# A decoder layer on one core: new byte offsets for six weight buffers in SBUF, and one buffer shared by two small tables

## The chip, the cores and the metric

The kernel runs on 1 NeuronCore of one Trainium2 chip. The metric is the device time of one execution in microseconds (us). The median of three runs of the kernel before is 2798.57 us (2797.53 to 2799.73).

## What is computed

One layer of a hybrid decoder on 512 tokens of width 2048, all in float32. Cut to what matters:

```python
mod = silu(c) @ w_ada + b_ada                      # six adaLN vectors of 2048
h = rmsnorm(x, g_mix) * (1 + sc1) + sh1
proj = h @ w_in                                    # 2048 x 11344
y_a = stick_breaking_attention(8 heads) @ w_a
y_b = dsa_attention(8 heads, top 128 keys by an indexer) @ w_b
x = x + (1 + gt1) * ((sigmoid(g_a) * y_a + sigmoid(g_b) * y_b) @ w_o)
h = rmsnorm(x, g_ffn) * (1 + sc2) + sh2
u = conv_b + causal depthwise conv of width 3 of (h @ w_up)     # 2048 x 11264
a, b = split(u)
x = x + (1 + gt2) * ((silu(a) * b) @ w_down)       # 5632 x 2048
out = rmsnorm(x, g_final)
```

## The kernel before

**Three matmuls for one product.** A float32 operand is split into a high part (rounded to the type `float32r` by a copy on ScalarE) and a low part (what is left, by a subtraction on VectorE). `mm3` (lines 164 to 168) then makes a product of two operands with three matmuls into the same PSUM tile: high by high (L166), high by low (L167), low by high (L168). Each matmul on TensorE (PE) has its own load of a stationary operand (LDWEIGHTS, the engine PEld in the profile) and streams a moving operand.

**The weights.** `load` (L143) brings 128 x 1024 elements of a weight matrix from HBM into one of eight `raw` buffers. `parts` (lines 152 to 159) splits it: L156 writes `wh`, L158 writes `wl`. There are three pairs of buffers, `wh0`/`wl0`, `wh1`/`wl1`, `wh2`/`wl2`; `turns` counts the calls of `parts` from 0, and call n uses pair n mod 3. A call's buffers are read by all matmuls of that block: 8 column groups of 128 for a block of 1024.

**The other operand.** Activations and what is formed of them lie in 62 slots named `F` of 512 elements (2048 bytes of each partition), split into high and low in the same way (L185, L187).

**Where the time is spent.** Most of the large matrix products run in `unit` (L230) with Strassen's scheme: two column blocks of 128 at a time, seven products in place of eight. One product is 8 blocks x 3 matmuls = 24 matmuls of 256 moving columns, `F` moving and a weight block of 128 x 128 stationary, and takes one call of `parts`. 31 units do most of the input projection, 8 the output projection `w_o`, 41 the up-projection `w_up`; the first part of the up-projection (`plain`, L1126) has the same matmuls at its own lines 1132 to 1134. Other products stream 512 columns: `proj` and the indexer's queries with the weights stationary, the values (L467 and `values`, L687) and the down-projection (`plain_down`, `strassen_down`) with the weights moving.

**Order.** Each engine runs its instructions in program order. ScalarE makes the high parts, the evacuations of PSUM and activation functions; VectorE makes the low parts, Strassen's sums and the adaLN products; SyncE issues the weight loads; GpSimd issues the saves and fetches of intermediate tiles.

**The layout in SBUF.** Tiles of the pool `sb` get their places in the order in which their tags are first seen, and each tile's room is a multiple of 32 bytes. The tables, the `F` slots and the `raw` buffers have sizes that are multiples of 128 bytes and all start at 0 modulo 128. Lines 127 to 140 ask for small tiles and weight buffers in turn, and so place the latter:

```python
eps = sb.tile([P, 1], F32, tag="eps", name="eps")       # 32 bytes of room
t2k("wh0", 1, F32R, 1024)                                # 32 modulo 128
inv = sb.tile([64, 1], F32, tag="inv", name="inv")      # 32 bytes
t2k("wh1", 1, F32R, 1024)                                # 64
sb.tile([P, NQB], F32, tag="r0", name=nm("r"))          # 32 bytes
t2k("wh2", 1, F32R, 1024)                                # 96
c_col = sb.tile([P, KT], F32, tag="c_col", name="c_col")  # 64 bytes
t2k("wl0", 1, F32R, 1024)                                # 32
...
```

and so on: `wl1` lies at 64 and `wl2` at 0. Modulo 128 bytes, and taken from the `F` slots, pair 0 lies at 32 (high) and 32 (low), pair 1 at 64 and 64, pair 2 at 96 and 0. A column group of 128 elements is 512 bytes and half an `F` slot is 1024 bytes, so every stationary block and every moving block starts at its buffer's offset modulo 128.

**The two small tables.** `macc` (L124) collects the adaLN sums, written by `ada_half` (L307) and read last by `ada_end` (L320) near the end of the output projection. `cw` (L123) holds the convolution's weights; its one DMA is issued from ScalarE's queue (L1105), and `conv` (L1108) reads it in the up-projection.

Of the kernel before, what the change touches and what calls it, by code (L numbers as in the profile page):

```python
# [10 lines left out]
F32 = mybir.dt.float32  # L11
F32R = mybir.dt.float32r
# [6 lines left out]
P = 128  # L19
# [57 lines left out]
def block_kernel(ctx: ExitStack, tc: tile.TileContext, A: dict, out: bass.AP):  # L77
    nc = tc.nc
    sb = ctx.enter_context(tc.tile_pool(name="sb", bufs=1))
    pp = ctx.enter_context(tc.tile_pool(name="pp", bufs=1, space=PSUM))  # L80
    dr = ctx.enter_context(tc.tile_pool(name="dr", bufs=1, space=bass.MemoryType.DRAM))

# [2 lines left out]
    def nm(s):  # L85
        counter[0] += 1
        return f"{s}_{counter[0]}"
# [4 lines left out]
    def slot(dt=F32):  # L92

        return t2k("F", SLOTS, dt)
# [14 lines left out]
    stt = nc.vector.scalar_tensor_tensor  # L109


    def small_r():
        counter[0] += 1
        return sb.tile([P, NQB], F32, tag=f"r{counter[0] % 2}", name=nm("r"))

    const = sb.tile([P, 5, P], F32, tag="const", name="const")
    ident, ones, negones, negtri, causal = (const[:, i, :] for i in range(5))
    vec = sb.tile([P, 96 + 2 * KT], F32, tag="vec", name="vec")
# [1 line left out]
    b_ada = vec[:, :96]  # L120
    g_mix, g_ffn = (vec[:, 96 + i * KT : 96 + (i + 1) * KT] for i in range(2))
    mask = sb.tile([P, 2, P], BF16, tag="mask", name="mask")
    cw = sb.tile([P, 2 * NJ, 4], F32, tag="cw", name="cw")  # L123
    macc = sb.tile([P, 96, 2], F32, tag="macc", name="macc")  # L124
    mod = sb.tile([P, 96], F32, tag="mod", name="mod")
    amp = sb.tile([P, 2, KT], F32, tag="amp", name="amp")
    slot()
    eps = sb.tile([P, 1], F32, tag="eps", name="eps")
    nc.vector.memset(eps, EPS)
    t2k("wh0", 1, F32R, 1024)  # L130
    inv = sb.tile([64, 1], F32, tag="inv", name="inv")
    t2k("wh1", 1, F32R, 1024)
    sb.tile([P, NQB], F32, tag="r0", name=nm("r"))
    t2k("wh2", 1, F32R, 1024)
    c_col = sb.tile([P, KT], F32, tag="c_col", name="c_col")
    t2k("wl0", 1, F32R, 1024)
    sb.tile([P, NQB], F32, tag="r1", name=nm("r"))
    t2k("wl1", 1, F32R, 1024)
    sb.tile([P, NQB], F32, tag="m", bufs=2, name=nm("m"))
    t2k("wl2", 1, F32R, 1024)  # L140


    def load(src, w=1024):  # L143
# [4 lines left out]
    pins = {}  # L148

    turns = [0]  # L150

    def parts(raw, w=1024):
        i = turns[0] % 3
        turns[0] += 1
        wh = t2k(f"wh{i}", 1, F32R, w)
        pins["wh"] = act(wh, raw, AF.Copy)  # L156
        wl = t2k(f"wl{i}", 1, F32R, w)
        pins["wl"] = tt(wl, raw, wh.bitcast(F32), ALU.subtract)  # L158
        return wh, wl

# [142 lines left out]
        return c1, c2  # L303

    def ada_half(cb, t, half, tag=("raw", 8)):  # L307
        raw = t2k(*tag, w=1024)
# [35 lines left out]
        return cb  # L344

    cb = c_spread()
    nc.scalar.dma_start(c_col, A["c_col"])
    act(c_col, c_col, AF.Silu)


    def rms(squares, blocks=range(NQB), bank=outs):

        total = bank()
        at = slice(blocks[0] * P, (blocks[-1] + 1) * P)
        for b in blocks:
            for i, t in enumerate(squares):
                mm(total[:, b : b + 1], t[:, b * P : (b + 1) * P], ones[:, :1], start=b == blocks[0] and i == 0,
                   stop=i == len(squares) - 1, skip_group_check=True)
        r = small_r()
        rb = r[:, blocks[0] : blocks[-1] + 1]  # L360
        act(rb, total[:, blocks[0] : blocks[-1] + 1], AF.Sqrt, scale=1.0 / D, bias=eps)
        nc.vector.reciprocal(rb, rb)
        wide = t2k("T", 2)
        for b in blocks:
            ts(wide[:, b * P : (b + 1) * P], ident, r[:, b : b + 1], None, ALU.mult)
        yield
        out = bank()
        mm(out[:, at], ones, wide[:, at], start=True, stop=True)
        yield out
# [138 lines left out]

    def rope_tables():
        f0, f1, f2, f3, f123, f23, fr = _turn_parts()  # L510
        nc.scalar.dma_start(inv, A["inv_freq"])
        pos = t2k("T", 2, I32)[:64]
        nc.scalar.dma_start(pos, A["positions"].to_broadcast([64, S]))
        turn = [t2k("w", 2)[:64] for _ in range(2)]

        def nearest(o, i, step):
            m = 1.5 * 2.0**23 * step
            ts(o, i, m, m, ALU.add, ALU.subtract)

        for half in range(2):  # L520
            at = slice(half * HALF, (half + 1) * HALF)
            q1, q2 = (t[:, at] for t in turn)
            tmp = sb.tile([P, 5 * HALF], F32, tag="soft", name=nm("soft"))[:64]
            ang, a2, a1, a0, rn = (tmp[:, i * HALF : (i + 1) * HALF] for i in range(5))
            nc.vector.tensor_copy(ang, pos[:, at])
            ts(ang, ang, inv, None, ALU.mult)
            nearest(a2, ang, 2.0**20)
            tt(ang, ang, a2, ALU.subtract)
            yield
            nearest(a1, ang, 2.0**8)  # L530
            tt(ang, ang, a1, ALU.subtract)
            nearest(a0, ang, 2.0**-4)
            tt(ang, ang, a0, ALU.subtract)
            small = ang
            ts(small, ang, fr, None, ALU.mult)
            yield
            stt(small, a0, f123, small, ALU.mult, ALU.add)
            stt(small, a1, f23, small, ALU.mult, ALU.add)
            stt(small, a2, f3, small, ALU.mult, ALU.add)
            ts(q1, a1, f0, None, ALU.mult)  # L540
            stt(q1, a2, f1, q1, ALU.mult, ALU.add)
            yield
            nearest(rn, q1, 1.0)
            tt(q1, q1, rn, ALU.subtract)
            ts(q2, a1, f1, None, ALU.mult)
            stt(q2, a2, f2, q2, ALU.mult, ALU.add)
            nearest(rn, q2, 1.0)
            tt(q2, q2, rn, ALU.subtract)
            yield
            stt(q1, a0, f0, q1, ALU.mult, ALU.add)  # L550
            tt(q1, q1, q2, ALU.add)
            nearest(rn, q1, 1.0)
            tt(q1, q1, rn, ALU.subtract)
            tt(q1, q1, small, ALU.add)
            yield
            nearest(rn, q1, 1.0)
            tt(q2, q1, rn, ALU.subtract)
            ts(q1, q2, 0.25, None, ALU.add)
            nearest(rn, q1, 1.0)
            tt(q1, q1, rn, ALU.subtract)  # L560
            yield
        TWO_PI = float(np.nextafter(np.float32(2 * np.pi), np.float32(0)))
        q1, q2 = turn
        for n, step in enumerate((64, 32)):
            o = t2k("raw", 8, w=1024)
            for i in range(P // step):
                at = slice(step * i, step * i + step)
                act(o[at, :S], q1[:step], AF.Sin, scale=TWO_PI)
                act(o[at, S:], q2[:step], AF.Sin, scale=TWO_PI if i % 2 else -TWO_PI)
                if i % 2:  # L570
                    yield
            save(rope_d[n], o)
# [140 lines left out]
    def indexer():  # L713
# [6 lines left out]
        for b in range(NQB):  # L720
            nc.tensor.transpose(wps[:, b * IDXH : (b + 1) * IDXH], tail[IDXD:TN, b * P : (b + 1) * P],
                                ident[IDXD:TN, IDXD:TN])
        wi = sb.tile([P, NQB, IDXH], F32, tag="wi", name="wi")
        nc.vector.tensor_copy(wi.rearrange("p b h -> p (b h)"), wps[:, : NQB * IDXH])
        bias.extend(slot()[:, : (b + 1) * P] for b in range(1, NQB))
        yield
# [36 lines left out]
        for b in range(1, NQB):  # L763
            sc = bias[b]
            for i in range(TOPK // 8):
                m8 = sb.tile([P, 8], F32, tag="m8", bufs=2, name=nm("m8"))
                nc.vector.max(out=m8, in_=sc)
                nc.vector.match_replace(out=sc, in_to_replace=m8, in_values=sc, imm_value=TAKEN)
                if i % 2:
                    yield  # L770
            ts(sc, sc, TAKEN, NEG, ALU.not_equal, ALU.mult)
# [127 lines left out]
    ya = [split(o) for o in ya]  # L899

    def sparse_1(q, k):
        m = sb.tile([P, NQB], F32, tag="m", bufs=2, name=nm("m"))
        s = sb.tile([P, NQB], F32, tag="s", bufs=2, name=nm("s"))
        soft = sb.tile([P, 10 * P], F32, tag="soft", name=nm("soft"))
        lg = strips(*(acc() for _ in range(3)))
        p = strips(*of_soft(soft))
# [125 lines left out]
    def norm_late(c1, c2):  # L1032
# [1 line left out]
        c, sq = (c1, c2), (t2k("ta", 2), t2k("sp", 2))  # L1034
        total, rstd = att(), outs()
        wide = t2k("T", 2)
        r = small_r()

        def add_up(t, blocks, first=False):
            for b in blocks:  # L1040
# [60 lines left out]
    rstd, finish_left, *left_norm = norm2  # L1101


    with behind(sig):
        nc.scalar.dma_start(cw, A["conv"])  # L1105
    yd = [dr.tile([P, 2 * S], F32, tag=f"yd{j}", name=f"yd{j}") for j in range(NJ // 2)]
# [349 lines left out]
        return [fetch(x1t[:, t, b * S : (b + 1) * S]) for b in range(2, 4)]  # L1456

    def finish_tokens(t, xs, s):
        r = small_r()
        tt(r[:, :2], s[:, :2], s[:, 2:], ALU.add)  # L1460
        tt(r[:, 2:3], r[:, :1], r[:, 1:2], ALU.add)
        act(r[:, 3:], r[:, 2:3], AF.Sqrt, scale=1.0 / D, bias=eps)  # L1462
        nc.vector.reciprocal(r[:, 3:], r[:, 3:])
        for b, x in enumerate(xs):
            if t == NQB - 1 and b < 2:
                act(x, x, AF.Copy, scale=r[:, 3:])
            else:
                stt(x, x, r[:, 3:], g_row[b], ALU.mult, ALU.mult)  # L1468
            nc.sync.dma_start(out[t][:, b * S : (b + 1) * S], x)
# [3 lines left out]
    for t in range(NQB):  # L1473
        ahead = operands(t + 1) if t + 1 < NQB else None
        xs = []
        s = sb.tile([P, NQB], F32, tag="s", bufs=2, name=nm("s"))
        for b in range(4):
            if not ps:
                ps = bank(t)
# [126 lines left out]
```

## Time and profile before

| | us |
|---|---|
| median of three runs | 2798.57 |
| the profiled execution's own time | 2800.61 |
| its span, first to last instruction | 2798.8 |
| PE busy / PEld busy | 2744.3 / 2500.2 |
| DVE busy / ACT busy / POOL busy | 2414.1 / 1455.4 / 314.7 |

The engines are named PE (TensorE's matmuls), PEld (its weight loads), DVE (VectorE), ACT (ScalarE), POOL (GpSimd) and SP (SyncE). Matmuls are pipelined: one begins about 0.12 us after another but is shown as busy for 0.28 us, so a busy PE is not one at its peak, and the rate is read from the distance of starts or from the count of matmuls in a stretch. All times within the execution count from the start of the span. Names in the rows leave buffer numbers out: `wh` is any of the three.

### The profile page before, as it was taken

The page shows a single profiled execution, that of the slowest core. Times are in us where ns is not written, and L with a number is a line of the kernel's source. Part 1 is how long each engine was busy: PE and PEld are TensorE (multiplying, and loading weights), DVE is VectorE, ACT ScalarE, POOL GpSimd, SP SyncE. Part 2 cuts the span into 40 slices and gives each one's busy share as a digit, 9 for nine tenths or more (in the row PEclk, how much of TensorE's full clock was granted, in tenths as well). Part 3 has the DMA queues.
Part 4 walks back from the last instruction along what each step waited for, and adds up shares of the span by engine and source line. Part 5 has one row for each costly group of instructions (what it writes and reads, how often), then busy time and mean ns, then how long its engine had stood idle before and what let it go on. Part 6 is the DMA issues. An engine that isn't in the chain of part 4 may idle for free. (4 is left out here: it accounts for less than half of the span.)

```text
span 2798.8 us, 47704 instructions
## 1 busy us (share of the span) xinstructions
PE 2744.3 (98%) x18704; PEld 2500.2 (89%) x18704; DVE 2414.1 (86%) x3452; ACT 1455.4 (52%) x2045; POOL 314.7 (11%) x519
## 2 busy tenths in 40 slices
PE   8999999999999999999999999999999999999996
PEld 6779999999998768889999999999999998887875
DVE  8978989988897899788888998989898887888886
ACT  4544454455556655434566555555555455446452
POOL 0100000001012111111220100000000000002112
PEclk9999999999999999999999999999999999999998
DMA  9973546655566448766773566666665436559686
GB/s 342 358 250 115 170 170 201 221 177 178 187 200 216 147 166 306 242 216 191 231 234 115 183 172 177 170 177 172 173 173 161 130 124 226 155 166 246 190 245 188
DMA packets 164189, 550.08 MB, mean 197 GB/s; under 512 B 21414, under 2 KB 21798, under 8 KB 163964
## 3 DMA queue, kind: packets, MB, share of 16 engines
q1 hardware_dynamic: 116220, 405.34, 45.1%
q0 software_dynamic: 47152, 141.30, 17.9%
q8 instruction: 147, 2.41, 0.3%
q14 instruction: 78, 0.64, 0.1%
q10 hardware_dynamic: 592, 0.39, 0.1%
HBM read 453.71 MB, written 89.83 MB: 194 GB/s over the span
## 5 line engine op out<-in xcount | busy, mean ns | idle before, releaser
L156 ACT ACTIVATE wh<-raw 128x1024 fp32r<-128x1024 f32 (+2 forms) x792 | 833.5, 1054 | 998.5 <-DVE raw L260 182.3
L158 DVE TENSOR_TENSOR wl<-raw,wh 128x1024 fp32r<-128x1024 f32 (+2 forms) x792 | 953.6, 1210 | 138.6 <-ACT wh L156 130.7
L166 PE MATMUL acc<-F,wh 128*128 128x256 f32 (+1 forms) x2464 | 714.5, 292 | 11.8 <-ACT wh L156 8.2
L168 PE MATMUL acc<-F,wl 128*128 128x256 f32 (+1 forms) x2464 | 716.8, 291 | 3.1 <-DVE wl L158 3.1
L167 PE MATMUL acc<-F,wh 128*128 128x256 f32 (+1 forms) x2464 | 715.3, 290 | 0.0
L168 PE MATMUL att<-F,wl 128*128 128x256 f32 (+1 forms) x2448 | 710.8, 290 | 1.7 <-DVE wl L158 1.7
L167 PE MATMUL att<-F,wh 128*128 128x256 f32 (+1 forms) x2448 | 710.5, 290 | 1.2 <-DVE F L187 1.2
L166 PE MATMUL att<-F,wh 128*128 128x256 f32 (+1 forms) x2448 | 709.3, 291 | 2.2 <-DVE sp L296 1.9
L166 PEld LDWEIGHTS acc<-F,wh 128*128 128x128 f32 x2464 | 462.6, 188 | 29.6 <-ACT wh L156 11.7
L168 PEld LDWEIGHTS acc<-F,wl 128*128 128x128 f32 x2464 | 463.7, 188 | 15.0 <-DVE wl L158 4.5
L166 PEld LDWEIGHTS att<-F,wh 128*128 128x128 f32 x2448 | 460.7, 188 | 14.8 <-issue 2.9
L167 PEld LDWEIGHTS acc<-F,wh 128*128 128x128 f32 x2464 | 462.7, 188 | 11.8 <-DVE F L407 0.5
L167 PEld LDWEIGHTS att<-F,wh 128*128 128x128 f32 x2448 | 460.5, 188 | 13.5 <-DVE F L187 4.3
L168 PEld LDWEIGHTS att<-F,wl 128*128 128x128 f32 x2448 | 461.8, 189 | 11.4 <-DVE wl L158 2.4
L310 DVE SCALAR_TENSOR_TENSOR raw<-raw,raw 128x1024 f32<-128x1024 f32 x152 | 181.8, 1215 | 0.3 <-DMA raw<-in_w_ada 0.2
L166 PE MATMUL att<-wh,F 128*128 128x512 f32 x448 | 180.0, 402 | 0.2 <-ACT wh L156 0.2
L167 PE MATMUL att<-wl,F 128*128 128x512 f32 x448 | 176.6, 394 | 0.8 <-DVE wl L158 0.8
L168 PE MATMUL att<-wh,F 128*128 128x512 f32 x448 | 177.3, 396 | 0.0
L256 DVE TENSOR_TENSOR raw<-raw,raw 128x1024 f32<-128x1024 f32 x80 | 97.2, 1216 | 34.7 <-DMA raw<-in_w_o 19.1
L167 PE MATMUL acc<-wl,F 128*128 128x512 f32 x288 | 114.6, 398 | 2.7 <-DVE wl L158 2.6
L168 PE MATMUL acc<-wh,F 128*128 128x512 f32 x288 | 114.1, 396 | 0.0
L166 PE MATMUL acc<-wh,F 128*128 128x512 f32 x288 | 113.4, 396 | 0.0
(364 smaller groups left out, 3618.1 us busy)
## 6 DMA issues: line engine op xcount, KB each, us to landing
raw<-in_w_up SPq DMA_DIRECT2D x164, 512.0 KB, 3.9
raw<-in_w_ada SPq DMA_DIRECT2D x152, 512.0 KB, 5.5
raw<-in_w_x SPq DMA_DIRECT2D x128, 512.0 KB, 4.3
raw<-in_w_down SPq DMA_DIRECT2D x104, 512.0 KB, 5.4
xd<-F POOLq DMA_DIRECT2D x64, 256.0 KB, 2.6
F<-xd POOLq DMA_DIRECT2D x64, 256.0 KB, 4.7
raw<-in_w_o SPq DMA_DIRECT2D x32, 512.0 KB, 5.3
soft<-in_w_gate SPq DMA_DIRECT2D x32, 512.0 KB, 4.0
```

The lines of the kernel that those rows point to most:

```text
L156: pins["wh"] = act(wh, raw, AF.Copy)
L158: pins["wl"] = tt(wl, raw, wh.bitcast(F32), ALU.subtract)
L166: mm(ps, ah, bh, start=first, stop=False, skip_group_check=not check)
L167: mm(ps, ah, bl, start=False, stop=False, skip_group_check=not check)
L168: return mm(ps, al, bh, start=False, stop=last, skip_group_check=not check)
L256: last_v = tt(s, a21, a22, ALU.add)
L310: return stt(raw, raw, 1.0, cb[half], ALU.mult, ALU.mult, accum_out=macc[:, t, half : half + 1])
```

## The change

The six weight buffers get rooms of 1,056 elements (4,224 bytes, 33 x 128) in place of 1,024, and `parts` uses 1,024 elements of them that begin at element 20, 24 or 28: 80, 96 or 112 bytes into the room. Both buffers of a pair have the same offset: pair 0 lies at 80, pair 1 at 96 and pair 2 at 112 bytes modulo 128. The small tiles go to a pool of their own, `tiny`, after `sb`, so nothing in `sb` has a size that is not a multiple of 128 bytes. `cw` takes the tag of `macc`, whose room grows from 768 to 1,408 bytes: the convolution's weights lie where the adaLN sums were, and their DMA can be issued only when the last sum has been read. The `r` tiles share one tag with two buffers in place of two tags taken by a counter's parity. No arithmetic changes, and no instruction is added or taken out in the code.

```diff
--- before.py
+++ after.py
@@ -77,6 +77,7 @@
 def block_kernel(ctx: ExitStack, tc: tile.TileContext, A: dict, out: bass.AP):
     nc = tc.nc
     sb = ctx.enter_context(tc.tile_pool(name="sb", bufs=1))
+    tiny = ctx.enter_context(tc.tile_pool(name="tiny", bufs=1))
     pp = ctx.enter_context(tc.tile_pool(name="pp", bufs=1, space=PSUM))
     dr = ctx.enter_context(tc.tile_pool(name="dr", bufs=1, space=bass.MemoryType.DRAM))
 
@@ -108,10 +109,6 @@
     ts = nc.vector.tensor_scalar
     stt = nc.vector.scalar_tensor_tensor
 
-
-    def small_r():
-        counter[0] += 1
-        return sb.tile([P, NQB], F32, tag=f"r{counter[0] % 2}", name=nm("r"))
 
     const = sb.tile([P, 5, P], F32, tag="const", name="const")
     ident, ones, negones, negtri, causal = (const[:, i, :] for i in range(5))
@@ -120,24 +117,8 @@
     b_ada = vec[:, :96]
     g_mix, g_ffn = (vec[:, 96 + i * KT : 96 + (i + 1) * KT] for i in range(2))
     mask = sb.tile([P, 2, P], BF16, tag="mask", name="mask")
-    cw = sb.tile([P, 2 * NJ, 4], F32, tag="cw", name="cw")
-    macc = sb.tile([P, 96, 2], F32, tag="macc", name="macc")
-    mod = sb.tile([P, 96], F32, tag="mod", name="mod")
-    amp = sb.tile([P, 2, KT], F32, tag="amp", name="amp")
-    slot()
-    eps = sb.tile([P, 1], F32, tag="eps", name="eps")
+    eps = tiny.tile([P, 1], F32, tag="eps", name="eps")
     nc.vector.memset(eps, EPS)
-    t2k("wh0", 1, F32R, 1024)
-    inv = sb.tile([64, 1], F32, tag="inv", name="inv")
-    t2k("wh1", 1, F32R, 1024)
-    sb.tile([P, NQB], F32, tag="r0", name=nm("r"))
-    t2k("wh2", 1, F32R, 1024)
-    c_col = sb.tile([P, KT], F32, tag="c_col", name="c_col")
-    t2k("wl0", 1, F32R, 1024)
-    sb.tile([P, NQB], F32, tag="r1", name=nm("r"))
-    t2k("wl1", 1, F32R, 1024)
-    sb.tile([P, NQB], F32, tag="m", bufs=2, name=nm("m"))
-    t2k("wl2", 1, F32R, 1024)
 
 
     def load(src, w=1024):
@@ -148,13 +129,18 @@
     pins = {}
 
     turns = [0]
+    PHASE = (80, 96, 112)
+
+    def weight_room(tag, w, dt=F32R):
+        i = turns[0] % 3
+        at = PHASE[i] // 4
+        return t2k(f"{tag}{i}", 1, dt, 1024 + 32)[:, at : at + w]
 
     def parts(raw, w=1024):
-        i = turns[0] % 3
         turns[0] += 1
-        wh = t2k(f"wh{i}", 1, F32R, w)
+        wh = weight_room("wh", w)
         pins["wh"] = act(wh, raw, AF.Copy)
-        wl = t2k(f"wl{i}", 1, F32R, w)
+        wl = weight_room("wl", w)
         pins["wl"] = tt(wl, raw, wh.bitcast(F32), ALU.subtract)
         return wh, wl
 
@@ -303,6 +289,9 @@
         return c1, c2
 
 
+    macc = sb.tile([P, 2 * NJ * 4], F32, tag="macc", name="macc")[:, : 192].rearrange("p (t h) -> p t h", h=2)
+    mod = sb.tile([P, 96], F32, tag="mod", name="mod")
+    amp = sb.tile([P, 2, KT], F32, tag="amp", name="amp")
 
     def ada_half(cb, t, half, tag=("raw", 8)):
         raw = t2k(*tag, w=1024)
@@ -344,6 +333,7 @@
         return cb
 
     cb = c_spread()
+    c_col = tiny.tile([P, KT], F32, tag="c_col", name="c_col")
     nc.scalar.dma_start(c_col, A["c_col"])
     act(c_col, c_col, AF.Silu)
 
@@ -356,7 +346,7 @@
             for i, t in enumerate(squares):
                 mm(total[:, b : b + 1], t[:, b * P : (b + 1) * P], ones[:, :1], start=b == blocks[0] and i == 0,
                    stop=i == len(squares) - 1, skip_group_check=True)
-        r = small_r()
+        r = tiny.tile([P, NQB], F32, tag="r", bufs=2, name=nm("r"))
         rb = r[:, blocks[0] : blocks[-1] + 1]
         act(rb, total[:, blocks[0] : blocks[-1] + 1], AF.Sqrt, scale=1.0 / D, bias=eps)
         nc.vector.reciprocal(rb, rb)
@@ -508,6 +498,7 @@
 
     def rope_tables():
         f0, f1, f2, f3, f123, f23, fr = _turn_parts()
+        inv = tiny.tile([64, 1], F32, tag="inv", name="inv")
         nc.scalar.dma_start(inv, A["inv_freq"])
         pos = t2k("T", 2, I32)[:64]
         nc.scalar.dma_start(pos, A["positions"].to_broadcast([64, S]))
@@ -720,7 +711,7 @@
         for b in range(NQB):
             nc.tensor.transpose(wps[:, b * IDXH : (b + 1) * IDXH], tail[IDXD:TN, b * P : (b + 1) * P],
                                 ident[IDXD:TN, IDXD:TN])
-        wi = sb.tile([P, NQB, IDXH], F32, tag="wi", name="wi")
+        wi = tiny.tile([P, NQB, IDXH], F32, tag="wi", name="wi")
         nc.vector.tensor_copy(wi.rearrange("p b h -> p (b h)"), wps[:, : NQB * IDXH])
         bias.extend(slot()[:, : (b + 1) * P] for b in range(1, NQB))
         yield
@@ -763,7 +754,7 @@
         for b in range(1, NQB):
             sc = bias[b]
             for i in range(TOPK // 8):
-                m8 = sb.tile([P, 8], F32, tag="m8", bufs=2, name=nm("m8"))
+                m8 = tiny.tile([P, 8], F32, tag="m8", bufs=2, name=nm("m8"))
                 nc.vector.max(out=m8, in_=sc)
                 nc.vector.match_replace(out=sc, in_to_replace=m8, in_values=sc, imm_value=TAKEN)
                 if i % 2:
@@ -899,8 +890,8 @@
     ya = [split(o) for o in ya]
 
     def sparse_1(q, k):
-        m = sb.tile([P, NQB], F32, tag="m", bufs=2, name=nm("m"))
-        s = sb.tile([P, NQB], F32, tag="s", bufs=2, name=nm("s"))
+        m = tiny.tile([P, NQB], F32, tag="m", bufs=2, name=nm("m"))
+        s = tiny.tile([P, NQB], F32, tag="s", bufs=2, name=nm("s"))
         soft = sb.tile([P, 10 * P], F32, tag="soft", name=nm("soft"))
         lg = strips(*(acc() for _ in range(3)))
         p = strips(*of_soft(soft))
@@ -1034,7 +1025,7 @@
         c, sq = (c1, c2), (t2k("ta", 2), t2k("sp", 2))
         total, rstd = att(), outs()
         wide = t2k("T", 2)
-        r = small_r()
+        r = tiny.tile([P, NQB], F32, tag="r", bufs=2, name=nm("r"))
 
         def add_up(t, blocks, first=False):
             for b in blocks:
@@ -1101,6 +1092,7 @@
     rstd, finish_left, *left_norm = norm2
 
 
+    cw = sb.tile([P, 2 * NJ, 4], F32, tag="macc", name="cw")
     with behind(sig):
         nc.scalar.dma_start(cw, A["conv"])
     yd = [dr.tile([P, 2 * S], F32, tag=f"yd{j}", name=f"yd{j}") for j in range(NJ // 2)]
@@ -1456,7 +1448,7 @@
         return [fetch(x1t[:, t, b * S : (b + 1) * S]) for b in range(2, 4)]
 
     def finish_tokens(t, xs, s):
-        r = small_r()
+        r = tiny.tile([P, NQB], F32, tag="r", bufs=2, name=nm("r"))
         tt(r[:, :2], s[:, :2], s[:, 2:], ALU.add)
         tt(r[:, 2:3], r[:, :1], r[:, 1:2], ALU.add)
         act(r[:, 3:], r[:, 2:3], AF.Sqrt, scale=1.0 / D, bias=eps)
@@ -1473,7 +1465,7 @@
     for t in range(NQB):
         ahead = operands(t + 1) if t + 1 < NQB else None
         xs = []
-        s = sb.tile([P, NQB], F32, tag="s", bufs=2, name=nm("s"))
+        s = tiny.tile([P, NQB], F32, tag="s", bufs=2, name=nm("s"))
         for b in range(4):
             if not ps:
                 ps = bank(t)
```

## The prediction

> **What bounds the kernel now.** I read the page, then the busy time by stretches, the waits, the matmuls by shape, and last the matmuls in order of time. From the page:
>
> ```profile
> span 2798.8 us, 47704 instructions
> ...
> PE 2744.3 (98%) x18704; PEld 2500.2 (89%) x18704; DVE 2414.1 (86%) x3452; ACT 1455.4 (52%) x2045; POOL 314.7 (11%) x519
> ```
>
> PE is shown busy throughout, but a matmul's busy time overlaps that of the next, so the share says nothing of its rate. Stretches do (busy us and instructions of PE, PEld, DVE, ACT and POOL, the granted clock, the DMA share, GB/s): the values' projection, the up-projection, the down-projection.
>
> ```profile
> 115.00:200.00 85.00, 85.00 (x368) 67.53 (x367) 68.61 (x117) 41.23 (x55) 7.55 (x14) 1.00 0.83 301
> 1600.00:1800.00 200.00, 200.00 (x1704) 200.00 (x1704) 181.02 (x213) 112.11 (x141) 14.31 (x21) 1.00 0.64 175
> 2400.00:2600.00 200.00, 198.35 (x852) 159.07 (x851) 165.69 (x201) 103.57 (x132) 28.64 (x34) 1.00 0.70 193
> ```
>
> In the second, PE is never idle and the clock is whole. Two of its 1,704 matmuls only reach in from before, so 1,702 begin in 200 us: 117.5 ns from one start to the next, with 256 columns each. In the third, with 512 columns, it is 198.35 us / 850 = 233 ns. The longest wait of PE's matmuls, in total over the whole span, is this one (us, times, the longest):
>
> ```profile
> PE acc L166 <- ACT wh L156: 8.2, 3, 7.0
> ```
>
> The operands are nearly always there before PE wants them. So the time is the number of matmuls times the distance of their starts. The change adds and removes none of them; it can only change the distance, and the question is whether the place of the weights enters into that.
>
> **How many matmuls.** By shape, one row of each kind that reads a weight buffer; the first is one of six alike (L166, L167, L168, to `acc` and `att`), the next of three, three, six and three:
>
> ```profile
> L166 PE MATMUL att<-F,wh 128*128 128x256 f32 x2240 | 629.0, 281 | 2.1 <-DVE sp L296 1.9 <-ACT wh L156 0.2
> ...
> L166 PE MATMUL att<-wh,F 128*128 128x512 f32 x448 | 180.0, 402 | 0.2 <-ACT wh L156 0.2
> ...
> L167 PE MATMUL acc<-wl,F 128*128 128x512 f32 x288 | 114.6, 398 | 2.7 <-DVE wl L158 2.6
> ...
> L167 PE MATMUL att<-F,wh 128*128 128x512 f32 x208 | 83.8, 403 | 1.2 <-DVE F L187 1.2
> ...
> L168 PE MATMUL outs<-wh,F 128*128 128x512 f32 x96 | 38.0, 396 | 0.5 <-DVE F L457 0.5
> ```
>
> With 256 columns: 6 x 2,240 = 13,440, or 560 products of 24, 186.7 for each of the three pairs (the few at lines 1132 to 1134 are left out). With 512: 3 x (448 + 288 + 96) + 6 x 208 = 3,744, or 156 blocks of 24, 52 for each pair.
>
> **The place of the weights shows in the distance.** Calls of `parts` are counted from the top of the program, from 0. The product that begins at 1701.49 us has call 444, so pair 0 (444 is 148 x 3); the one at 1709.95 has call 447, again pair 0; that at 1712.79 has pair 1, that at 1715.54 pair 2, and at 1718.41 pair 0 is back.
>
> ```profile
> 1701.49 0.28 PE L166 MATMUL att<-F,wh 128*128 128x256 f32 x1
> ...
> 1709.95 0.28 PE L166 MATMUL acc<-F,wh 128*128 128x256 f32 x1
> ...
> 1712.79 0.28 PE L166 MATMUL acc<-F,wh 128*128 128x256 f32 x1
> ...
> 1713.50 0.28 PE L166 MATMUL acc<-F,wh 128*128 128x256 f32 x1
> ...
> 1715.43 0.28 PE L168 MATMUL acc<-F,wl 128*128 128x256 f32 x1
> 1715.54 0.28 PE L166 MATMUL acc<-F,wh 128*128 128x256 f32 x1
> ...
> 1718.41 0.28 PE L166 MATMUL acc<-F,wh 128*128 128x256 f32 x1
> ```
>
> Three equal products of 24 matmuls take 2.84, 2.75 and 2.87 us: 118.3 ns a matmul with pair 0 (offsets 32 and 32 from the moving operand modulo 128), 114.6 with pair 1 (64 and 64), 119.6 with pair 2 (96 and 0). The product's own kind does not make the difference: seven products make a unit and three pairs take turns, so each pair meets each kind; and the three products before, of other kinds, took 1709.95 - 1701.49 = 8.46 us, to the hundredth what these three took. Inside pair 1's product the distance settles. The first six matmuls take 0.71 us (118 ns each); the 17 from 1713.50 to 1715.43 take 1.93 us, 113.5 ns each. My reading is that the load of the next stationary block and the stream of the moving one read SBUF at the same time and get into each other's way, more or less by the difference of their offsets.
>
> With 512 columns and the weights moving, four blocks' first matmuls, calls 18 to 21, pairs 0, 1, 2 and 0:
>
> ```profile
> 114.55 0.39 PE L166 MATMUL outs<-wh,F 128*128 128x512 f32 x1
> ...
> 120.15 0.39 PE L166 MATMUL outs<-wh,F 128*128 128x512 f32 x1
> ...
> 125.67 0.40 PE L166 MATMUL outs<-wh,F 128*128 128x512 f32 x1
> ...
> 131.25 0.39 PE L166 MATMUL outs<-wh,F 128*128 128x512 f32 x1
> ```
>
> 5.60, 5.52 and 5.58 us: the same order, but 0.08 us between best and worst in blocks twice as long.
>
> **The change part by part.** *The offsets.* The new ones are 80, 96 and 112, the same for both buffers of a pair. The trace has 64 on one side, and 96 only beside 0; 80 and 112 it doesn't show. So each new pair is bounded by the best and the worst rows. Below: the settled distance from the first matmul on, 24 x 113.5 ns = 2.724 us a product. Above: pair 2's 2.87. I take pair 1's 2.75 for all three, for two reasons. Pair 1 is the only one of the three with both buffers in the upper half of the 128 bytes, where all the new ones lie. And the first load from offset 96, at the end of pair 1's product, lets the next matmul begin 0.11 us later (1715.43 to 1715.54), no later than in the settled run; what makes pair 2 the worst may then be its 0, or the change between two offsets within every three matmuls, which a pair with one offset doesn't have. Against it stands pair 0, which has one offset and doesn't settle: one offset is not enough. Pair 0's products then gain 0.09 us and pair 2's 0.12: 186.7 x 0.21 = 39.2 us. For the 512 columns, where the new differences are 48, 32 and 16 with the weights moving, I take nothing; the bounds are 52 x (0.08 + 0.06) = 7.3 us gained if all were like the best, and 52 x (0.08 + 0.02) = 5.2 us lost if all were like the worst.
>
> A gain on PE must not be eaten by the engines that feed it. DVE is the next: 181 us busy in 200, so a product set faster by 39.2 / (560 x 2.82) = 2.5% leaves it at 93%. It would be late only if the distance fell by over 9%, or if its own work at the new offsets took a tenth longer; that costs nothing now because PE's stream covers it.
>
> The Trainium skill, "TensorE: Matmul & The Clock Gate", section "Step-by-step: what each phase is for", says that PE has two independent read ports and that loading the next weights takes no read bandwidth from the running matmul; "SBUF — State Buffer", section "Who interferes with whom", says that PE never waits on anyone. By that the offsets would be worth nothing and the sum would be 0. The rows of 2.84, 2.75 and 2.87 us don't agree with it as it stands.
>
> *The shared buffer.* The rows of `cw` (its first reader, its load) and of `macc`'s last readers (least, median and longest ns, then the first and the last start):
>
> ```profile
> L1110 ACT ACTIVATE w<-F,cw x88: 795/802/830, 1505.4 to 2327.5; 128x512 f32<-128x512 f32 x88
> ...
> L1105 ACTq DMA_DIRECT2D cw<-in_conv x1: 334/334/334, 861.8 to 861.8; - x1
> ```
>
> ```profile
> L326 DVE TENSOR_TENSOR mod<-macc x2: 166/175/184, 831.2 to 1403.8; 128x16 f32<-128x16 f32 x1, 128x32 f32<-128x32 f32 x1
> ```
>
> The load moves from 861.8 us to some place after 1403.8, and has until 1505.4. It is 0.33 us of issue on ACT, half idle there. Queued behind it on ACT would be the copies that make `wh`; its wait is for a VectorE instruction that is long done if the load stands where the code has it, after the output projection. I cost it at nothing, hidden by the 100 us between; without them it would cost its issue and its landing, a few us, once. The tags of `r` and the pool of small tiles move no instruction: nothing, from either side.
>
> *The sum.* The profiled execution took 2800.61 us, 2.04 above the median of 2798.57. 2800.61 - 39.2 = 2761.4, and by the median 2798.57 - 39.2 = 2759.4: I say 2759.
>
> **The rivals.** *A: the settled run from the start.* If all three new offsets settle at once, products take 2.724 us: (0.116 + 0.026 + 0.146) x 186.7 = 53.8 us, so 2745, and 2737 with the 512 columns' 7.3. For it: 113.5 ns holds once it is reached. Against: pair 1 needs six matmuls for it after another pair, and the pairs still differ.
>
> *B: no change.* Either the three new offsets happen to have the old mean of 2.82 us a product, one between 64 and 96, one at 96, one between 96 and 0; or the distance hangs on something else that goes around with the pairs. For it: plain interpolation between the rows gives about this, if 96 by itself is as bad as pair 2. 2799. The two sections of the Trainium skill named above would have it so by the second way.
>
> *C: slower.* The offset 96 itself is what makes pair 2 the worst: its high part is read by two matmuls of three. Then 96 and its neighbours 80 and 112 all run like pair 2, and the one good offset, 64, is gone: (0.03 + 0.12) x 186.7 = 28 us more, 2827. It decides from the point where the mean of the three new pairs is above 2.82 us a product. For it: pair 2's row. Against: the single step of 0.11 us.
>
> **How the numbers follow.** Forecast 0.45, with a range of its own of 2747 to 2774; A 0.17; B 0.13; C 0.25, spread between 2805 and 2827 as one, two or three pairs lose. The range goes from A with the 512 columns' best, 2737, over B to the middle of C's price, 2812: it leaves out half of C and a little of A. About 0.2%, 5.6 us, is what a measurement can tell from no change: faster by more 0.62, within it 0.13, slower by more 0.25.
>
> **What would show it.** Right: the same count of matmuls, over 1,740 of them in 200 us of the up-projection, three products in a row within 0.03 us of one another near 2.75, and PE still without idle time there. A: products near 2.72. C: a product with call number 1 modulo 3, offset 96, at 2.87 or above. Wrong in another way: PE idle before L166 or L168 with ACT or DVE as the releaser in the up-projection, or the load of `cw` with the copies of `wh` waiting behind it.

## The result and the profile after

| | before | after |
|---|---|---|
| median, us | 2799.15 | 2815.27 |
| lowest to highest of four runs, us | 2797.53 to 2800.46 | 2814.28 to 2816.91 |
| profiled execution, us | 2800.61 | 2814.28 |

The ratio of the times is 1.0064 (95% interval 1.0052 to 1.0077): the change costs about 16 us by the medians. The forecast was 2759, with a range from 2737 to 2812.

From the page of the kernel after:

```profile
span 2812.5 us, 47708 instructions
...
PE 2754.8 (98%) x18704; PEld 2512.3 (89%) x18704; DVE 2415.8 (86%) x3452; ACT 1453.6 (52%) x2045; POOL 313.4 (11%) x519
```

The span is 13.7 us longer. PE has the same 18,704 matmuls and is busy for 10.5 us more (2754.8 against 2744.3); what is left of the span, its idle time, went from 54.5 to 57.7 us, 3.2 more. So most of the loss is in the matmuls themselves. The busy time by stretches of the kernel after, in the columns used before:

```profile
0.00:160.00 160.00, 140.70 (x573) 110.24 (x574) 140.21 (x254) 72.44 (x100) 8.54 (x20) 0.97 0.92 338
1600.00:1800.00 200.00, 200.00 (x1694) 200.00 (x1693) 180.26 (x212) 112.41 (x143) 14.90 (x21) 1.00 0.65 173
2400.00:2600.00 200.00, 199.00 (x851) 159.47 (x850) 164.79 (x201) 105.46 (x136) 29.69 (x36) 1.00 0.69 188
```

In the up-projection 1,692 matmuls begin in 200 us (two of the 1,694 reach in): 118.2 ns apart, where before had 117.5. Over 13,440 matmuls 0.7 ns is 9.4 us. PE is never idle there, in the one kernel or the other. The products in order of time in the kernel after; the row at 1700.65 is the first matmul of a product with pair 1, those after it begin products with pairs 2, 0, 1, 2 and 0:

```profile
1700.65 0.28 PE L152 MATMUL att<-F,wh 128*128 128x256 f32 x1
...
1703.50 0.28 PE L152 MATMUL att<-F,wh 128*128 128x256 f32 x1
...
1706.31 0.28 PE L152 MATMUL att<-F,wh 128*128 128x256 f32 x1
...
1709.16 0.28 PE L152 MATMUL att<-F,wh 128*128 128x256 f32 x1
...
1711.98 0.28 PE L152 MATMUL att<-F,wh 128*128 128x256 f32 x1
...
1714.85 0.28 PE L152 MATMUL att<-F,wh 128*128 128x256 f32 x1
```

96 bytes took 2.85 us, 112 took 2.81, 80 took 2.85, 96 again 2.82 and 112 again 2.87. So one offset does not have one time: the five products lie between 2.81 and 2.87 us, and none is at 2.75.

The other part of the loss is at the start. In the first 160 us, 573 matmuls run after, 594 before:

```profile
0.00:160.00 160.00, 145.87 (x594) 113.27 (x595) 144.50 (x260) 74.98 (x103) 9.79 (x20) 0.99 0.94 345
```

The 600th matmul begins 5.1 us later than in the trace of before. Of the waits in the first 110 us, this one of PE, in the kernel after, stands out:

```profile
PE acc L152 <- ACT F L396: 6.6, 1, 6.6
```

In the kernel before the same wait is short:

```profile
PE acc L166 <- ACT F L406: 0.5, 1, 0.5
```

In the kernel after, SyncE's DMA queue has a wait that before doesn't have:

```profile
SPq L298 <- PE att L154: 5.6, 1, 5.6
```

The timeline of the kernel after around it:

```profile
3.96 0.65 SPq L298 DMA_DIRECT2D wh<-in_w_ada  x1
...
19.17 0.39 PE L154 MATMUL att<-F,wl 128*128 128x512 f32 x1
...
19.36 0.33 SPq L298 DMA_DIRECT2D wh<-in_w_ada  x1
...
25.35 0.72 ACT L396 ACTIVATE F<-F,amp 128x512 fp32r<-128x512 f32 x1 [6.57 <-DVE amp L394]
```

And that of the kernel before, where both loads of this kind were issued together:

```profile
4.00 1.84 SPq L309 DMA_DIRECT2D wh<-in_w_ada  x2
```

The adaLN's second tile borrows `wh1` and `wh2` for its own weights. Before, the first call of `parts` took pair 0, and both were free. The diff moves `turns[0] += 1` ahead of the line that picks the pair, so that call 0 takes pair 1. One of the two loads can then be issued only when the matmuls of call 0 have read `wh1`, 15 us later, and `amp`, the copy to `F` and PE wait for it in turn.

### The profile page after: what moved, and what is told of

Same layout as the page of the kernel before. It is cut to its first block, busy times and chain, and to the rows that moved or that the text cites. A ratio compares the mean times of both kernels' runs of the same rounds, so it can differ in the third digit from the quotient of the medians.

```text
span 2812.5 us, 47708 instructions
## 1 busy us (share of the span) xinstructions
PE 2754.8 (98%) x18704; PEld 2512.3 (89%) x18704; DVE 2415.8 (86%) x3452; ACT 1453.6 (52%) x2045; POOL 313.4 (11%) x519
```

## The experiments

The dispute was over what makes the distance of the matmuls. The theory made after the result: it is the difference, modulo 128 bytes, between the place of the stationary weights and that of the moving operand, and only 64 lets the distance settle. The rivals: the new layout with the shared buffer of `cw` and `macc` costs the time by itself; or any one offset for all six buffers settles, and only the change from one offset to another disturbs. In each run the kernel before was timed beside it; its medians were 2798.66 us for the first four runs, 2798.02 for the next four and 2797.76 for the last four. Ratios are to these.

**Run 1: all at 64.**

```diff
-    PHASE = (80, 96, 112)
+    PHASE = (64, 64, 64)
```

> The changed kernel with all three pairs of weight buffers 64 bytes off the operand tiles modulo 128. Theory 1 (the difference of the offsets of the stationary and the moving block sets the distance of matmuls, and of the offsets so far only 64 lets it settle): no pair ever disturbs the settled run, so products of 24 matmuls in the up-projection take about 2.72 us, 13,440 x (117.5 - 113.5 ns) = 54 us less than the kernel before: about 2745 us, with some us either way from the matmuls of 512 columns. Theory 2 (something else of the new layout costs the time: the order of the buffers in SBUF, or the table that shares the sums' buffer): about 2815 us as the changed kernel. Theory 3 (one offset for all three pairs settles, whatever it is; what costs is the step from pair to pair): 2745 us too.

2765.01 us, ratio 0.988 (0.9866 to 0.9893). The up-projection of this run:

```profile
1600.00:1800.00 200.00, 200.00 (x1768) 200.00 (x1767) 187.97 (x222) 114.78 (x147) 14.70 (x21) 1.00 0.64 179
```

1,766 starts: 113.3 ns. Four products in order of time:

```profile
1701.39 0.28 PE L152 MATMUL acc<-F,wh 128*128 128x256 f32 x1
...
1704.11 0.28 PE L152 MATMUL acc<-F,wh 128*128 128x256 f32 x1
...
1706.83 0.28 PE L152 MATMUL acc<-F,wh 128*128 128x256 f32 x1
...
1709.55 0.28 PE L152 MATMUL acc<-F,wh 128*128 128x256 f32 x1
```

Each takes 2.72 us, whatever its pair. The time is 20 us above the 2745 that was expected: this kernel still has the wait at the start, PE is idle for 63.1 us (span 2759.1 less 2696.0 busy) against 54.5 before, and it is busy for 48.3 us less, not 54. With everything else of the change in place, the offset alone turned the loss into a gain, so neither the layout nor the shared buffer is the cause of the loss.

**Run 2: all at 96.** `PHASE = (96, 96, 96)`.

> The changed kernel with all three pairs at 96 bytes. Theory 1: 96 doesn't settle, products take 2.8 to 2.87 us as they did with pair 1 at 96 in the changed kernel: 2805 to 2825 us. Theory 2: 2815 us. Theory 3: 2745 us, products of 2.72 us.

2811.35 us, ratio 1.0045 (1.003 to 1.0061).

```profile
1600.00:1800.00 200.00, 200.00 (x1701) 200.00 (x1700) 180.82 (x214) 112.57 (x143) 14.92 (x21) 1.00 0.63 173
```

1,699 starts, 117.7 ns. One offset for all pairs is not enough: that theory falls. It also bears on rival C of the prediction: 96 by itself gives 117.7, not the 119.6 of pair 2.

**Run 3: the old offsets in the new layout.**

```diff
-    PHASE = (80, 96, 112)
+    PHASE = {"wh": (32, 64, 96), "wl": (32, 64, 0)}
...
-        at = PHASE[i] // 4
+        at = PHASE[tag][i] // 4
```

> The changed kernel, its layout and its shared buffer, with the offsets of the kernel before: high parts at 32, 64 and 96, low parts at 32, 64 and 0. Theory 1: as the kernel before, 2799 us within 3, products of 2.84, 2.75 and 2.87 us. Theory 2: 2815 us. Theory 3: 2799 us.

2800.17 us, ratio 1.0007 (0.9998 to 1.0016): the old offsets give the old time back.

```profile
1600.00:1800.00 200.00, 200.00 (x1713) 200.00 (x1712) 181.82 (x215) 113.96 (x145) 14.91 (x21) 1.00 0.65 176
```

116.9 ns, even a little below the 117.5 of before. This kernel still has the changed counter and the wait of SyncE's queue at the start, which the shorter distance seems to make up for; why the distance is 0.6 ns shorter isn't settled. The shared buffer can be seen to cost nothing directly too, in the rows of `cw` in the kernel after (its first reader, its load; least, median and longest ns, first and last start):

```profile
L1102 ACT ACTIVATE w<-F,cw x88: 797/801/833, 1512.3 to 2339.3; 128x512 f32<-128x512 f32 x88
...
L1097 ACTq DMA_DIRECT2D cw<-in_conv x1: 334/334/334, 1410.8 to 1410.8; - x1
```

The load is issued 101.5 us ahead of its first reader.

**Run 4: the difference or the place?** A pad of 64 bytes is put ahead of `macc`, so that the operand tiles that follow lie at 64 modulo 128, and the offset of 64 within the rooms then puts the weights at 0.

```diff
     mask = sb.tile([P, 2, P], BF16, tag="mask", name="mask")
+    nc.vector.memset(sb.tile([P, 16], F32, tag="pad", name="pad"), 0.0)
...
-    PHASE = (80, 96, 112)
+    PHASE = (64, 64, 64)
```

> All tiles from the sums' buffer on begin 64 bytes later, so the operand slots lie at 64 and the weights, 64 bytes further, at 0 modulo 128. Theory 1 (the difference counts): as all at 64, products of 2.72 us, about 2745 us. If it is the stationary block's own place that counts, 64 is gone for the weights and the products take 2.8 us or more: 2800 us or more.

2760.34 us, ratio 0.9868 (0.9852 to 0.9883).

```profile
1600.00:1800.00 200.00, 200.00 (x1767) 200.00 (x1766) 187.79 (x222) 115.34 (x147) 15.58 (x22) 1.00 0.65 181
```

113.3 ns again, and the time is 15 us above the expected one as in run 1. What counts is the difference between the two operands, not where the weights lie.

The `raw` buffers move with the operand tiles here, so this run alone doesn't exclude that another engine's work on the weight buffers disturbs PE. The trace of the kernel before speaks against it: from 1622 to 1955 us, 119 products in a row, every product of pair 0 takes 2.833 to 2.834 us, of pair 1 2.755 and of pair 2 2.871 to 2.872, although each pair meets all seven kinds of product, with other work on VectorE and ScalarE beside them.

**Run 5: the counter put back.** The offsets of the change, and `turns` raised after the pair is chosen.

```diff
     def parts(raw, w=1024):
-        turns[0] += 1
         wh = weight_room("wh", w)
         pins["wh"] = act(wh, raw, AF.Copy)
         wl = weight_room("wl", w)
+        turns[0] += 1
```

> The changed kernel, offsets 80, 96 and 112, with the counter raised after the pair is taken, as in the kernel before, so that the first block of weights uses pair 0 and not pair 1, whose high buffer the adaLN's second tile borrows. In the changed kernel that tile's load waited 5.6 us for the first block's matmuls and the 600th matmul began 5.1 us late. Theory S (the start's loss is the counter's): the 600th matmul begins within 1 us of the kernel before and the time is 2810 us, 5 less than the changed kernel. Rival (the start's loss comes from the pool of small tiles or the order of the tiles): no change, 2815 us. The distance of matmuls in the up-projection stays at 118 ns by both.

2809.13 us, ratio 1.0039 (1.0025 to 1.0053), 6 us less than the change. Two stretches:

```profile
0.00:160.00 160.00, 146.68 (x596) 114.30 (x597) 145.13 (x262) 75.10 (x104) 9.55 (x21) 0.99 0.94 346
1600.00:1800.00 200.00, 200.00 (x1693) 200.00 (x1692) 180.39 (x212) 111.06 (x141) 15.29 (x22) 1.00 0.64 173
```

The first 160 us hold 596 matmuls in place of 573, and the distance stays at 118.3 ns. So the two losses are separate: the counter costs about 6 us (runs 6 and 1, which differ in the counter alone, are 8 us apart), the offsets alone 11 us (0.39% of 2798).

**Run 6: all at 64 with the counter put back.** Runs 1 and 5 together.

> All pairs at 64 and the counter as in the kernel before. If the two parts of the change are independent: 5 us less than with all at 64 and the changed counter, 2760 us; settled distance of 113.3 ns in the up-projection. Rival: the faster matmuls already wait for the weights or DVE elsewhere, so less than 3 us are gained: 2762 us or more.

2756.61 us, ratio 0.9852 (0.9839 to 0.9866): the fastest kernel of the study, 41 us below the one before and 59 below the change. From its page, and its up-projection:

```profile
span 2757.8 us, 47705 instructions
...
PE 2695.3 (98%) x18704; PEld 2454.1 (89%) x18704; DVE 2410.0 (87%) x3452; ACT 1449.8 (53%) x2045; POOL 313.9 (11%) x519
```

```profile
1600.00:1800.00 200.00, 200.00 (x1767) 200.00 (x1767) 187.99 (x222) 114.76 (x148) 14.70 (x21) 1.00 0.64 179
```

PE is busy for 49.0 us less than before, near the 53.8 that rival A of the prediction had worked out for it. But its idle time rose from 54.5 to 62.5 us. With PE faster, VectorE's operands are late for longer; two of the waits of this kernel's matmuls:

```profile
PE acc L154 <- DVE wl L144: 5.3, 4, 2.7
PE att L152 <- DVE sp L282: 4.4, 4, 2.0
```

and the same two before:

```profile
PE acc L168 <- DVE wl L158: 3.1, 4, 1.2
...
PE att L166 <- DVE sp L296: 1.9, 2, 1.4
```

These two rows have grown by 4.7 of the 8.0 us.

**Runs 7 and 8: all at 80, all at 112** (with the changed counter; each timed once).

> All pairs at 80, the changed counter. Theory 1 as it stands leaves 80 open: if the distance settles near 64 only, 118 ns in the up-projection and about 2815 us; if pair 0's 118.4 ns in the changed kernel were owed to its neighbours at 96 and 112, 113.3 ns and about 2765 us.

> All pairs at 112, the changed counter. If the distance of matmuls with 256 columns settles near 64 only: 118 ns and about 2810 us, with the blocks of 512 columns that have the weights stationary at 228 ns as for pair 2 of the changed kernel; if the neighbours matter: 113.3 ns and 2765 us.

2804.66 and 2818.14 us. The up-projection at 80:

```profile
1600.00:1800.00 200.00, 200.00 (x1701) 200.00 (x1700) 180.86 (x213) 112.77 (x143) 14.90 (x21) 1.00 0.64 175
```

and at 112:

```profile
1600.00:1800.00 200.00, 200.00 (x1688) 200.00 (x1687) 179.48 (x210) 111.61 (x142) 14.90 (x21) 1.00 0.64 174
```

117.7 and 118.6 ns. All three of the change's offsets are on the slow side. The times missed the expected ones by 10 us down (80) and 8 us up (112), and the 228 ns expected at 112 for blocks of 512 columns with the weights stationary did not come either: the mean distance of their matmuls in the trace is 231.2. Runs 7, 2 and 8 have a mean of 2811.4 us; the change, which mixes the three, took 2815.27.

**Runs 9 and 10: 64 and 192 modulo 256.** A difference of 64 modulo 128 is 64 or 192 modulo 256, and the rooms of the change put some buffers at the one and some at the other (counted, as always here, from the operand slots). Here the six buffers get 4,096 bytes each, one after the other, and a pad ahead of them puts all at one place modulo 256; the slots that follow lie 128 bytes past a multiple of 256, so that a pad of 48 elements, 192 bytes, gives the difference 64. The counter is put back. Run 9; run 10 has the pads of 16 and 48 elements the other way round:

```diff
     mask = sb.tile([P, 2, P], BF16, tag="mask", name="mask")
+    sb.tile([P, 48], F32, tag="pad", name="pad")
+    for tag in ("wh", "wl"):
+        for i in range(3):
+            t2k(f"{tag}{i}", 1, F32R, 1024)
+    sb.tile([P, 16], F32, tag="pad2", name="pad2")
...
-        at = PHASE[i] // 4
-        return t2k(f"{tag}{i}", 1, dt, 1024 + 32)[:, at : at + w]
+        return t2k(f"{tag}{i}", 1, dt, 1024)[:, :w]
```

> The counter as in the kernel before; the six buffers lie one behind the other, 4,096 bytes each, all at 64 modulo 256. With all at 64 modulo 128 pair 2, whose two buffers lay at 192 modulo 256, had blocks of 512 columns with moving weights at 232.9 ns a matmul, pair 1, at 64 modulo 256, at 229.6. If the place modulo 256 counts for these blocks: some 800 x 3.3 ns for pair 2's and a little for pair 0's, 3 to 5 us less than all at 64 modulo 128 with the counter as before (2756.6 us): 2752 us. Rival (only the place modulo 128 counts, pair 2 differs by its position in the round): 2757 us, and pair 2 still at 232.9.

> The same with all six at 192 modulo 256. Modulo 256 counts: products of 256 columns still settle (113.3 to 114 ns), blocks of 512 columns with moving weights at 232.9 ns for all pairs, about 2762 us. Rival (modulo 128): as all at 64, 2757 us.

Run 9: 2761.16 us, ratio 0.9862 (0.9846 to 0.9879). Run 10: 2796.83 us, ratio 0.9989 (0.9968 to 1.001), with single runs from 2773.01 to 2802.18; its profile is of a run of 2782.79. Both expectations were missed, the second by far. Run 9, in two stretches of the input projection, in the up-projection and in the down-projection:

```profile
440.00:540.00 100.00, 100.00 (x885) 100.00 (x884) 93.59 (x135) 43.26 (x54) 5.94 (x11) 1.00 0.66 214
580.00:630.00 50.00, 50.00 (x427) 50.00 (x426) 44.26 (x54) 29.31 (x40) 3.77 (x7) 1.00 0.56 184
1600.00:1800.00 200.00, 200.00 (x1767) 200.00 (x1766) 186.95 (x221) 115.56 (x148) 14.14 (x20) 1.00 0.65 179
2400.00:2600.00 200.00, 197.94 (x859) 160.43 (x859) 167.33 (x203) 102.64 (x130) 30.44 (x36) 1.00 0.72 200
```

Run 10:

```profile
440.00:540.00 100.00, 100.00 (x852) 100.00 (x851) 91.74 (x132) 41.18 (x50) 5.40 (x10) 1.00 0.63 208
1600.00:1800.00 200.00, 200.00 (x1767) 200.00 (x1766) 186.18 (x220) 116.10 (x147) 15.03 (x21) 1.00 0.66 182
2400.00:2600.00 200.00, 198.88 (x848) 158.36 (x848) 162.51 (x197) 103.93 (x133) 28.67 (x34) 1.00 0.67 187
```

And run 6 in the first of these stretches:

```profile
440.00:540.00 100.00, 100.00 (x884) 100.00 (x884) 94.62 (x137) 43.32 (x53) 5.40 (x10) 1.00 0.66 216
```

In the up-projection both have 1,765 starts, 113.3 ns. In the input projection two distances occur, with PE never idle in any of these stretches. From 440 to 540 us run 10 has 850 starts, 117.6 ns, where run 9 has 883 and run 6 has 882, 113.3 and 113.4 ns. But run 9 too has stretches at 117.6: 425 starts from 580 to 630 us. So a difference of 64 modulo 128 allows the settled run and does not force it. In run 10 the matmuls come 113 ns apart before this wait and 117.7 ns apart after it:

```profile
263.12 0.38 PE L157 MATMUL acc<-F,wl 128*128 128x256 f32 x1 [0.74 <-DVE wl L147]
```

That distance then holds past 800 us. In run 6 two starts are 1.02 us apart at 566 us, as at this wait; there the distance is 117.7 ns for some 20 matmuls and then 113.3 again. What an execution loses seems to depend on the waits that it meets and on how soon it settles again. That run 10's spread from run to run comes from this is likely, but only one of its executions has a trace, and why run 6 settles again sooner, no run shows. Neither is better than run 6, whose rooms mix the two.

**Runs 11 and 12: all at 0, all at 48** (with the changed counter; each timed once).

> All pairs at 0 modulo 128, where the operand tiles lie, the changed counter. Theory 1 with nearness to 64 as what counts: the farthest, 118 to 119.5 ns in the up-projection and 2810 to 2825 us. If equal offsets of stationary and moving blocks were harmless: 113.3 ns, 2765 us.

> All pairs at 48, the changed counter: as far below 64 as 80 is above. If 64 is one good place with nothing on either side: 117 to 118 ns, 2805 to 2812 us as with 80. If what settles is a range from 48 to 64: 113.3 ns and 2765 us.

2818.51 and 2836.52 us. At 0:

```profile
1600.00:1800.00 200.00, 200.00 (x1682) 200.00 (x1681) 179.12 (x210) 111.05 (x142) 14.89 (x21) 1.00 0.63 173
```

and at 48:

```profile
1600.00:1800.00 200.00, 200.00 (x1665) 199.85 (x1664) 178.28 (x210) 110.67 (x141) 14.92 (x21) 1.00 0.63 173
```

119.0 and 120.3 ns. Run 12 missed both of its expectations: 48 is worse than 80, by 32 us. The offsets tried, in this stretch, in order: 0: 119.0; 48: 120.3; 64: 113.3; 80: 117.7; 96: 117.7; 112: 118.6 ns. There is no slope towards 64; it is the single good place among those tried, with the worst 16 bytes below it. 56, 72, 16 and all at 32 were not tried.

## Why the prediction was wrong

**Right: what bounds the kernel.** That the time is the number of matmuls times the distance of their starts, and that the place of the weights against the moving operand sets the distance, held in every run: by `PHASE` alone the time moved from 2765.01 (64) to 2836.52 us (48). The two sections of the Trainium skill named in the prediction ("Step-by-step: what each phase is for" of "TensorE: Matmul & The Clock Gate" and "Who interferes with whom" of "SBUF — State Buffer"), by which an offset is worth nothing, don't agree with the 113.3 to 120.3 ns of these runs.

**Wrong: "I take pair 1's 2.75 for all three."** This is the step that failed. It carried the whole sum of 39.2 us and turned its sign. The rows showed that 64 is good; I carried that over to 80, 96 and 112 because they lie in the same half of the 128 bytes. Measured, the products shown take 2.81 to 2.87 us; at 118.2 ns a matmul their mean is 2.84, above the 2.82 that they had to stay under. The good pair was the one that the change gave up, as rival C says.

**Wrong: the second reason.** The single step of 0.11 us at the load from offset 96 followed a settled run of pair 1. One step after a settled run says little of the pair that begins there: with all six buffers at 96 the distance is 117.7 ns. And the other half of that reason, a pair with one offset doesn't change between two within three matmuls, was already spoken against by pair 0's row of 2.84, as the prediction itself says.

**Rival C: right in kind, too dear.** The good offset was lost, but the new pairs don't run like pair 2 (119.6 ns); they run at 118.2 in the mean. So the offsets cost 11 us (run 5), not 28. The mechanism named for it, 96 as the cause of pair 2's 119.6, isn't borne out: 96 alone gives 117.7, 0 alone 119.0. Of rival B, the second way falls with run 1: by `PHASE` alone the distance went from 118.2 to 113.3 ns, so it does not hang on something else that goes around with the pairs.

**Missed: the order of two lines in `parts`.** The diff shows `turns[0] += 1` above the choice of the pair. I costed the new `parts` at nothing and wrote that offset 96 goes with call number 1 modulo 3; after the change it goes with 0 modulo 3. The queue that this holds up is SyncE's: 5.6 us behind call 0's matmuls, about 6 us in the whole time. This term was missing from the sum and from every rival; without it the change would have taken 2809 us (run 5), still a loss. To see it one has to list who else writes to `wh1`: the adaLN's second tile.

**Right: the small parts.** The shared buffer and the tiny tiles moved nothing that can be seen: run 3 with both is at 1.0007, though it also has the wait at the start and the shorter distance; the load of `cw` is early by 101.5 us. For the 512 columns I took nothing within bounds of 7.3 us gained and 5.2 lost; in the down-projection the change has 199.00 / 849 = 234.4 ns against 198.35 / 850 = 233.4 before, 1 ns, inside the bounds.

**Rival A** is what the change would have been with 64 in all three places: 2.72 us a product, as worked out. Its 2745 us lacked the waits that a faster PE uncovers, 8.0 us, and 4.8 us of matmul time (49.0 against 53.8); run 6 measured 2756.61.

## What to carry to other kernels

Where PE is never idle, compare the distance of equal matmuls by the buffer that they read; if it differs, the place in SBUF is a knob, and each value of it has to be measured, since a good place says nothing of its neighbours 16 bytes away. Before a rotating buffer's counter is touched, list everything else that borrows these buffers: a shift by one turn can put a load behind matmuls. And if a trace shows one good case among several, the plainest change is to give all the others that case's value: here that was run 6, 2756.61 us against 2815.27.

## What the runs showed of the hardware that was not expected

- With 128 x 128 stationary blocks and 256 moving columns, PE's matmuls can settle at 113.3 ns where weights and moving operand differ by 64 bytes modulo 128; at 0, 48, 80, 96 and 112 they run at 117.7 to 120.3 ns in the up-projection. Why 64 is the one, no run shows; that PE's two reads of SBUF get into each other's way is still a reading.
- At a difference of 64 the settled run can be lost and won back: before the change pair 1 reached it after six matmuls; in run 10 the same difference gave 117.6 ns in the input projection, from a wait of PE on, and 113.3 in the up-projection.
- With 512 columns and the weights moving, modulo 256 counts: the down-projection's matmuls are 197.94 / 857 = 231.0 ns apart in run 9 (64 modulo 256) and 198.88 / 846 = 235.1 ns in run 10 (192 modulo 256), each count less the two that reach in. Run 6, which mixes the two, lies between: 198.64 / 855 = 232.3 ns.
